# Query and key projections of ten heads in 512- and 256-column matmuls over four PSUM banks, in place of 256-column matmuls over two

## The chip, the core and the metric

The kernel runs on one core of one Trainium2 chip. The metric is device microseconds of one execution. The core has five engines that work side by side and meet through semaphores: TensorE (PE in the profile, with its weight loads as PEld) multiplies, VectorE (DVE) and ScalarE (ACT) do elementwise work, GpSimd (POOL) and SyncE (SP) mostly issue DMAs here. Matmul results land in PSUM, eight banks of 2 KB per partition (512 floats); the engines' working memory is SBUF.

## The reference, cut to what matters

Two layers over x of 256 tokens by 2048: a gated linear attention (GLA, 4 heads) and a retention layer (8 heads). Each projects the normalised input into q, k, values and gates, mixes along the tokens, normalises per head, multiplies by silu(gate), and projects back.

```python
proj = h @ w_in                       # GLA: 2048 -> 1024+1024+4096+4096, retention: 2048 -> 2048+2048+4096+4096
q, k, v, gate = jnp.split(proj, ...)
...                                   # rotary or decay, chunked scores, values, norm per head
return (o * jax.nn.silu(gate)) @ w_out   # 4096 -> 2048
h = h + mixer(rms_norm(h, norm))      # twice, then a final rms_norm
```

All inputs are float32 and the result must be accurate to about that. Nearly all of the time is these dense projections: some 320 MB of weights are read once.

## The kernel before, in words

**Precision by two halves.** Each float32 operand is split into a high half (rounded to the fp32r type of the fast matmul) and the rest. A product of two operands is then three fast matmuls: high by high, high by low, low by high. The activations live split in `xhl` (and `ogt` for the output projections): 16 blocks of 128 rows, each with a high and a low half of 256 tokens side by side, so 512 columns.

**The weight pipeline.** `_plan` lists all weight blocks in the order of use: a *sub* is 256 rows by 512 columns (512 KB, two 128-row blocks). SP loads a sub into one of 8 raw buffers; `emit_split` makes the halves, `hi` on ACT (L291) and `lo` on DVE (L292); both have 4 buffers, and the splits are issued 3 subs ahead of their use (`LOOK`).

**Pairs.** In many places two projections (a gate block g and a value block v of a head, or two neighbouring column blocks of an output projection) are computed together by a Strassen-like scheme, `pair` in the plan: quarter products P1, P2, P3, P5, P6, P7, P8, some on sums of activation blocks (`sums`, `rsum`, `osum`) and sums of weights, and plain steps v4 to v7 and g4 to g7. The sums of weights are made in the raw buffers: `post` entries of the plan are DMAs that POOL issues (L300) and that add another block onto a raw buffer after its split; `pre` entries are DVE additions (L286). A raw buffer x (g's blocks 0 and 1) serves P1, P5, P6 and P8, with additions between them; a buffer z (v's blocks 2 and 3) serves P6's sum, P3 and P7. After P6, x has g's blocks 2 and 3 added; after the later of P3 and P6, z has v's blocks 0 and 1 added. A product step P is two subs with 6 matmuls each, a plain step v or g one sub with 12.

**Orders.** A string gives the order of a pair's steps: `UNIT`, `LATE` for the first output pair of each retention half, and for the retention heads `WHOLE` (eight q steps, then UNIT; heads 0 and 4) or `MIXED` (q steps spread between the products; heads 1, 2, 3, 5, 6, 7). After each step, `turn` and `step` let one piece of the earlier head's work (`ret_tasks`: rotary, scores, values, norm, transposes) or of other side work into the program. The tile framework then lists every engine's instructions once, at build time, by its own estimate of when each is ready, so neighbouring steps can be interleaved; on the chip each engine runs its list in order.

**q and k.** A head's q and k blocks (4 column blocks of 128, numbered c) are computed transposed: the weights are the stationary operand, `xhl` the moving one. `step_w` does one sub: per 128-row block and c three matmuls of 256 columns (L365: weight high by x high; L366: weight high by x low; L368: weight low by x high), all into the same 256 columns of PSUM. So a head's q and k fill two banks (two c to a bank): for GLA heads two of the four `acc` banks (`group_w`, `evac_w`), for retention heads the two `lev` banks (`ret_head`, `qk_done`). One ACT copy of 128x512 per bank takes them out (L393, L1297). A retention pair uses the four `acc` banks as A (P1, P6, P7, P8, and the gates' second half), B (P2 and gates), C (values; in MIXED also P5) and V1 (values).

**What sets the order around the change.** In MIXED, P2 (into bank B) stands between q3 and q4. After q7 come the copies of q and k, the remaining tasks of the head before, then P3 (into C), v4, and so on.

Of the kernel before, what the change touches and what calls it, by code (L numbers as in the profile page):

```python
# [10 lines left out]
F32 = mybir.dt.float32  # L11
# [44 lines left out]
def _plan():  # L56


    loads, subs = [], []

    def load(gid, j):
        loads.append((gid, j))
        return len(loads) - 1

    def use(c, pre=None, post=()):
        subs.append((c, pre, post))

    def plain(gid, js=range(NSUB)):
        for j in js:
            use(load(gid, j))  # L70

    def pair(g, v, q=None, order=None):
        order = (order or UNIT).split()
        x = [load(g, 0), load(g, 1)] if order[0] == "P1" else []
        z = []
        later = max(("P3", "P6"), key=order.index)
        owed = []
        for n, tok in enumerate(order):
            kind, i = tok[0], tok[1:]
            if kind in "qvg":  # L80
                use(load({"q": q, "v": v, "g": g}[kind], int(i)), post=owed)
                owed = []
            elif tok == "z":
                z += [load(v, 2), load(v, 3)]
            elif tok == "P2":
                use(load(g, 2), post=owed)
                plain(g, [3])
                owed = []
            else:
                if tok == "P1" and not x:  # L90
                    x += [load(g, 0), load(g, 1)]
                for j in range(2):
                    post = []
                    if tok == later:
                        post.append((z[j], (v, j)))
                    if tok == "P1":
                        post.append((x[j], (v, j)))
                    if tok == "P6":
                        (owed if " ".join(order) == LATE else post).append((x[j], (g, 2 + j)))
                    use(z[j] if tok in ("P3", "P7") else x[j], z[j] if tok == "P6" else None, post)  # L100

    def out_cols_of(name, half, joint):
        for c in (0, 2):
# [49 lines left out]


def ret_order(h):
    return MIXED if h % 4 else WHOLE


EARLY = 2
# [10 lines left out]
def kernel(  # L170
# [17 lines left out]
    nc = tc.nc  # L188
# [9 lines left out]
    t4_p = pool("t4", 4)  # L198
# [5 lines left out]
    lev_p = pool("lev", 2, space=psum)  # L204
# [3 lines left out]
    mm = nc.tensor.matmul  # L208
    keep = tc.keep_in_program_order
# [130 lines left out]
    def steps_x(ps, lhs, js, hook=None, deadline=None):  # L340
        for j in js:
# [7 lines left out]
                hook(j)  # L349
            advance()  # L350

    def step_w(rhs, ps, j, given=True, early=False):
        hi, lo = next_weights()
        at = lambda c: ps[c // 2][:, c % 2, :]
        both = lambda c: {"skip_group_check": c % 2 == 1}
        order = [(q, c) for q in range(SUB) for c in range(4)]
        if j == NSUB - 1 or (j == 0 and given):
            order = [(q, c) for c in range(4) for q in range(SUB)]
        his, los = [], []
        for q, c in order:  # L360
            kt = j * SUB + q
            wh = hi[:, q, c * P : (c + 1) * P]
            wl = lo[:, q, c * P : (c + 1) * P]
            a = [
                lambda c=c, wh=wh, kt=kt: mm(at(c), wh, rhs[:, kt, 0, :], start=kt == 0 and c % 2 == 0, stop=False, **both(c)),  # L365
                lambda c=c, wh=wh, kt=kt: mm(at(c), wh, rhs[:, kt, 1, :], start=False, stop=False, **both(c)),  # L366
            ]
            b = [lambda c=c, wl=wl, kt=kt: mm(at(c), wl, rhs[:, kt, 0, :], start=False, stop=kt == NKT - 1, **both(c))]  # L368
            if not early:
                for x in a + b:  # L370
                    x()
                continue
            his += a
            los += b
            if c == 3:
                for x in his + los:
                    keep(x())
                his, los = [], []

    def group_w(rhs, name, extra=None, given=False):  # L380
        ps = acc(2, f"{name}_ps", (P, 2, SEQ))
# [12 lines left out]

    begun, closed = set(), set()

# [120 lines left out]
    xhl = const([P, NKT, 2, SEQ], "xhl", F32R)  # L517
# [320 lines left out]
    def gla_head(h):  # L838
        hw = {}
        if h > 1:  # L840
            side.appendleft(gla_decay(h, hw))
        ps = group_w(xhl, f"gqk{h}", None if h else first_group, h > 0)
# [6 lines left out]
        evac_w(ps, qk)  # L849
        hw["qk"] = qk  # L850
        if h == 0:
            side.append(gate_low_rank())
# [60 lines left out]
        for gi in range(2):  # L913
            g = 2 * h + gi
            if g in JOINT["a"]:
                v = v_p.tile([P, 2, 2, GW], F32R, tag="v", name=f"gv{g}")
# [4 lines left out]
                banks = [slots[n] for n in (1, 0, 2, 3)]  # L921
# [361 lines left out]
    def ret_head(h):  # L1283
        lhs = xhl
        mixed = h % 4 != 0
        at = (2, 3, 0, 1)
        q_ps = [lev_p.tile([P, 2, SEQ], F32, tag="lev", name=f"rqk{h}_ps{c}") for c in range(2)]
        r, r2 = r2_[:, 0, :], r2_[:, 1, :]
        box = {}

        def qk_done():
            if h == 0:
                token_norm(r2_, "n2")
                nc.vector.tensor_tensor(r2_[:, 1, :], r2_[:, 0, :], r2_[:, 0, :], ALU.mult)
            qk = t4_p.tile([P, 4, SEQ], F32, tag="qk", name=f"rqk{h}", bufs=1)
            for i in range(2):
                nc.scalar.activation(qk[:, 2 * i : 2 * i + 2, :], q_ps[i], AF.Copy)  # L1297
# [261 lines left out]
```

## Time and profile before

| | |
|---|---|
| median of 3 runs | 1383.21 us (1383.12 to 1383.39) |
| profiled execution, its own time | 1383.86 us |
| its span, first to last instruction | 1382.1 us, granted TensorE clock 0.998 |
| PE busy | 1369.5 us, 7376 matmuls |
| DVE busy | 1089.2 us |
| ACT busy | 847.8 us |
| POOL busy | 145.9 us |
| DMA | 321.42 MB, mean 233 GB/s |

The rows of the profile read so: the groups give line, engine, operation, tiles (out<-in), shapes and count, then busy us, mean ns of one, and idle time before them. Matmuls are pipelined, so a matmul's own length (283 ns for 256 columns) is longer than its step to the next one; the step is read from successive start times in the timeline. Timeline rows start with the start and the length in us; a bracket at the end is the idle time of that engine before the row, and what ended it. Rows of windows give the stretch, its length and each engine's busy time with the number of instructions.

### The profile page before, as it was taken

What the parts mean: (1) busy time and instruction counts of PE and PEld (TensorE: products, weight loads), DVE (VectorE), ACT (ScalarE), POOL (GpSimd) and SP (SyncE); (2) the same over time, 40 slices, a digit from 0 to 9 for tenths busy, and PEclk for the clock granted to TensorE, in tenths of its full rate; (3) what the DMA queues carried; (4) which work ended last, traced back from release to release, by engine and by line L of the source; (5) the groups of instructions that cost most, each with busy time, mean ns of one, the idle gap of its engine ahead of it and who ended that gap; (6) DMA issues with size and microseconds to landing.
All of it is one profiled execution on the core that took longest, in us unless ns stands there. A gap on an engine that the chain in (4) does not pass through costs nothing.

```text
span 1382.1 us, 19965 instructions
## 1 busy us (share of the span) xinstructions
PE 1369.5 (99%) x7376; PEld 1186.0 (86%) x7376; DVE 1089.2 (79%) x1481; ACT 847.8 (61%) x1098; POOL 145.9 (11%) x206
## 2 busy tenths in 40 slices
PE   9999999999999999999999999999999999999997
PEld 8888988888988988888989898988798989898887
DVE  6586795887778786768787888888857898987883
ACT  6576556656567756656666566665546666666662
POOL 1003020110021021001011010101101011110100
PEclk9999999999999999999999999999999999999999
DMA  9755556689658657868897879798898787979881
GB/s 345 257 182 155 182 160 196 145 253 337 210 153 257 198 175 184 318 168 240 270 328 181 270 200 282 202 329 215 243 382 222 245 237 225 261 219 280 234 291 71
DMA packets 85953, 321.42 MB, mean 233 GB/s; under 512 B 9936, under 2 KB 10960, under 8 KB 84320
## 3 DMA queue, kind: packets, MB, share of 16 engines
q1 hardware_dynamic: 66768, 240.55, 49.1%
q0 software_dynamic: 17648, 72.23, 25.0%
q10 hardware_dynamic: 1440, 7.38, 1.4%
q8 instruction: 58, 0.95, 0.3%
q14 instruction: 39, 0.32, 0.1%
HBM read 307.53 MB, written 12.58 MB: 232 GB/s over the span
## 4 chain that ended last, share of the span: by engine, by line
PE 94%; DMA 3%; DVE 1%; issue 1%; ACT 1%; POOL 0%; DVEq 0%; SPq 0%; ACTq 0%; POOLq 0%
PE re_ps L401 8%; PE re_ps L400 8%; PE re_ps L402 8%; PE rqk_ps L368 4%; PE rqk_ps L366 4%; PE rqk_ps L365 4%; DMA raw<-in_w_all 3%; PE gg_ps L332 3%; PE gv_ps L333 3%; PE gv_ps L329 3%; PE gv_ps L332 3%; PE gg_ps L329 3%; PE gg_ps L333 3%; PE gqk_ps L365 2%; PE gqk_ps L368 2%; PE gqk_ps L366 2%
## 5 line engine op out<-in xcount | busy, mean ns | idle before, releaser
L292 DVE TENSOR_TENSOR lo<-raw,hi 128x1024 fp32r<-128x1024 f32 (+1 forms) x569 | 688.7, 1221 | 222.1 <-ACT hi L291 216.6
L291 ACT ACTIVATE hi<-raw 128x1024 fp32r<-128x1024 f32 (+1 forms) x569 | 597.7, 1056 | 398.3 <-PE rqk_ps L366 61.0
L366 PE MATMUL rqk_ps<-xhl,hi 128*128 128x256 f32 x512 | 144.0, 283 | 0.0
L365 PE MATMUL rqk_ps<-xhl,hi 128*128 128x256 f32 x512 | 143.9, 283 | 0.0
L300 POOL DMA_DIRECT2D raw<-in_w_all x96 | 83.2, 867 | 547.1 <-DVE lo L292 302.7
L368 PE MATMUL rqk_ps<-xhl,lo 128*128 128x256 f32 x512 | 140.3, 283 | 0.0
L401 PE MATMUL re_ps<-lo,xhl 128*128 128x512 f32 x352 | 137.6, 391 | 0.0
L402 PE MATMUL re_ps<-hi,xhl 128*128 128x512 f32 x352 | 137.1, 389 | 0.0
L400 PE MATMUL re_ps<-hi,xhl 128*128 128x512 f32 x352 | 131.0, 390 | 0.0
L365 PEld LDWEIGHTS rqk_ps<-xhl,hi 128*128 128x128 f32 x512 | 97.9, 191 | 1.9
L366 PEld LDWEIGHTS rqk_ps<-xhl,hi 128*128 128x128 f32 x512 | 98.0, 191 | 1.4
L368 PEld LDWEIGHTS rqk_ps<-xhl,lo 128*128 128x128 f32 x512 | 96.0, 192 | 0.7
L402 PEld LDWEIGHTS re_ps<-hi,xhl 128*128 128x128 f32 x352 | 66.1, 188 | 13.3
L400 PEld LDWEIGHTS re_ps<-hi,xhl 128*128 128x128 f32 x352 | 66.2, 188 | 13.2
L401 PEld LDWEIGHTS re_ps<-lo,xhl 128*128 128x128 f32 x352 | 66.2, 188 | 12.6
L333 PE MATMUL gv_ps<-hi,xhl 128*128 128x512 f32 x192 | 75.5, 393 | 0.0
L332 PE MATMUL gg_ps<-lo,xhl 128*128 128x512 f32 x192 | 75.4, 393 | 0.0
L333 PE MATMUL gg_ps<-hi,xhl 128*128 128x512 f32 x192 | 75.0, 391 | 0.0
L332 PE MATMUL gv_ps<-lo,xhl 128*128 128x512 f32 x192 | 75.0, 391 | 0.0
L329 PE MATMUL gg_ps<-hi,xhl 128*128 128x512 f32 x192 | 74.9, 390 | 0.0
L329 PE MATMUL gv_ps<-hi,xhl 128*128 128x512 f32 x192 | 74.6, 391 | 0.0
L365 PE MATMUL gqk_ps<-xhl,hi 128*128 128x256 f32 x256 | 73.2, 289 | 1.3 <-ACT hi L291 1.3
(430 smaller groups left out, 2841.0 us busy)
## 6 DMA issues: line engine op xcount, KB each, us to landing
raw<-in_w_all SPq DMA_DIRECT2D x447, 512.0 KB, 5.2
raw<-in_w_all POOLq DMA_DIRECT2D x96, 512.0 KB, 7.5
resid<-in_x_n SPq DMA_DIRECT2D x2, 1024.0 KB, 9.5
gg<-in_gn_g POOLq DMA_DIRECT2D x8, 256.0 KB, 4.2
resid_x<-resid ACTq DMA_DIRECT2D x1, 2048.0 KB, 10.6
gb<-in_gn_b POOLq DMA_DIRECT2D x8, 256.0 KB, 7.0
gb_resid<-resid_x POOLq DMA_DIRECT2D x1, 2048.0 KB, 11.8
resid_g<-gb_resid ACTq DMA_DIRECT2D x1, 2048.0 KB, 8.8
```

Of the source, the lines that this page charges most:

```text
L291: a = nc.scalar.activation(hi[:, sl], src[:, sl], AF.Copy)
L292: b = nc.vector.tensor_tensor(lo[:, sl], src[:, sl], hi[:, sl].bitcast(F32), ALU.subtract)
L300: nc.gpsimd.dma_start(raws[n], block(key), accum_op=ALU.add)
L329: first_mm = mm(ps, xh, hi[:, q, :], start=kt == 0, stop=False)
L332: mm(ps, xh, lo[:, q, :], start=False, stop=False)
L333: mm(ps, xl, hi[:, q, :], start=False, stop=kt == NKT - 1)
L365: lambda c=c, wh=wh, kt=kt: mm(at(c), wh, rhs[:, kt, 0, :], start=kt == 0 and c % 2 == 0, stop=False, **both(c)),
L366: lambda c=c, wh=wh, kt=kt: mm(at(c), wh, rhs[:, kt, 1, :], start=False, stop=False, **both(c)),
L368: b = [lambda c=c, wl=wl, kt=kt: mm(at(c), wl, rhs[:, kt, 0, :], start=False, stop=kt == NKT - 1, **both(c))]
L400: mm(ps, xh, hi[:, q, :], start=start, stop=False, **again)
L401: mm(ps, xh, lo[:, q, :], start=False, stop=False, **again)
L402: mm(ps, xl, hi[:, q, :], start=False, stop=stop, **again)
```

## The change

It has four parts.

1. `step_w` uses the 512 columns of `xhl` (x high and x low) in one matmul with the high weights, and one matmul of 256 columns with the low weights. The result of each c is then two halves of one bank that have to be added, so q and k take four banks. This holds for all four GLA heads and retention heads 0, 1, 3, 4, 5, 7. `step_both` is the former three-matmul form, kept for retention heads 2 and 6 (`compact`).
2. The four banks: GLA head 0 takes all four `acc` banks, GLA heads 1 to 3 two `acc` and the two `lev` banks, retention heads 0 and 4 the `lev` banks, C and V1, retention heads 1, 3, 5, 7 the `lev` banks, V1 (c = 2) and B (c = 3). The evacuation is now, for each c, an ACT copy of the second half (128x256) into a `t4` tile and a DVE addition of the first half (128x256).
3. The orders: in heads 1, 3, 5, 7 (MIXED) P2 moves behind q7, because it uses B. Heads 2 and 6 keep the former string under the name SPREAD.
4. In the plan, the additions onto x after P6 are put off until the next step's first split (`owed`) in all output pairs of the retention layer; before, in the LATE pairs only. This changes one pair, the second of the first half.

```diff
                     if tok == "P6":
-                        (owed if " ".join(order) == LATE else post).append((x[j], (g, 2 + j)))
+                        (owed if v[0] == "ro" else post).append((x[j], (g, 2 + j)))
...
-MIXED = "q0 q1 P1 q2 q3 P2 q4 z P5 q5 P6 q6 q7 P3 v4 v5 v6 P7 v7 g4 g5 P8 g6 g7"
+MIXED = "q0 q1 P1 q2 q3 q4 z P5 q5 P6 q6 q7 P2 P3 v4 v5 v6 P7 v7 g4 g5 P8 g6 g7"
+SPREAD = "q0 q1 P1 q2 q3 P2 q4 z P5 q5 P6 q6 q7 P3 v4 v5 v6 P7 v7 g4 g5 P8 g6 g7"
...
-    return MIXED if h % 4 else WHOLE
+    return (WHOLE, MIXED, SPREAD, MIXED)[h % 4]
...
+    def step_both(rhs, ps, j):
+        hi, lo = next_weights()
...
+            mm(at, wh, rhs[:, kt, 0, :], start=kt == 0 and c % 2 == 0, stop=False, **more)
+            mm(at, wh, rhs[:, kt, 1, :], start=False, stop=False, **more)
+            mm(at, wl, rhs[:, kt, 0, :], start=False, stop=kt == NKT - 1, **more)
     def step_w(rhs, ps, j, given=True, early=False):
...
+            if kt == NKT - 1:
+                mm(ps[c][:, 0, :], wl, rhs[:, kt, 0, :], start=False, stop=False)
+                mm(ps[c], wh, rhs[:, kt, :, :], start=False, stop=True)
+            else:
+                mm(ps[c], wh, rhs[:, kt, :, :], start=kt == 0, stop=False)
+                mm(ps[c][:, 0, :], wl, rhs[:, kt, 0, :], start=False, stop=False)
...
+    def group_w(rhs, name, extra=None, ps=None):
+        given = ps is not None
+        ps = ps or acc(4, f"{name}_ps", (P, 2, SEQ))
...
-    def evac_w(ps, dst):
+    def evac_w(ps, dst, name):
+        tmp = t4_p.tile([P, 4, SEQ], F32, tag="t4", name=f"{name}_h2")
         with tc.high_priority():
-            for i in range(2):
-                to = dst[:, i, :].rearrange("p (z k t) -> p k z t", z=2, k=2)
-                nc.scalar.activation(to, ps[i].rearrange("p k (z t) -> p k z t", z=2), AF.Copy)
+            for c in range(4):
+                nc.scalar.activation(tmp[:, c, :], ps[c][:, 1, :], AF.Copy)
+                halves = lambda a: a.rearrange("p (z t) -> p z t", z=2)
+                to = dst[:, c // 2, :].rearrange("p (z k t) -> p z k t", z=2, k=2)[:, :, c % 2, :]
+                nc.vector.tensor_tensor(to, halves(ps[c][:, 0, :]), halves(tmp[:, c, :]), ALU.add)
...
+        if h > 0:
+            banks = acc(2, f"gqk{h}_ps", (P, 2, SEQ))
+            banks += [lev_p.tile([P, 2, SEQ], F32, tag="lev", name=f"gqk{h}_ps{c}") for c in (2, 3)]
...
+        compact = h % 4 == 2
         q_ps = [lev_p.tile([P, 2, SEQ], F32, tag="lev", name=f"rqk{h}_ps{c}") for c in range(2)]
+        if not compact:
+            more = (3, 1) if mixed else (2, 3)
+            q_ps += [acc(1, f"rqk{h}_ps{n}", (P, 2, SEQ), [at[n]])[0] for n in more]
...
-            for i in range(2):
-                nc.scalar.activation(qk[:, 2 * i : 2 * i + 2, :], q_ps[i], AF.Copy)
+            if compact:
+                for i in range(2):
+                    nc.scalar.activation(qk[:, 2 * i : 2 * i + 2, :], q_ps[i], AF.Copy)
+            else:
+                tmp = t4_p.tile([P, 4, SEQ], F32, tag="t4", name=f"rqk{h}_h2")
+                for c in range(4):
+                    nc.scalar.activation(tmp[:, c, :], q_ps[c][:, 1, :], AF.Copy)
+                    nc.vector.tensor_tensor(qk[:, c, :], q_ps[c][:, 0, :], tmp[:, c, :], ALU.add)
...
-            step_w(lhs, q_ps, j)
+            (step_both if compact else step_w)(lhs, q_ps, j)
```

More of the change, by code (lines that the diff above doesn't have):

```diff
@@ L350, in steps_x @@
             advance()
+    def step_both(rhs, ps, j):
+        hi, lo = next_weights()
+        order = [(q, c) for q in range(SUB) for c in range(4)]
+        if j in (0, NSUB - 1):
+            order = [(q, c) for c in range(4) for q in range(SUB)]
+        for q, c in order:
+            kt = j * SUB + q
+            at, more = ps[c // 2][:, c % 2, :], {"skip_group_check": c % 2 == 1}
+            wh = hi[:, q, c * P : (c + 1) * P]
+            wl = lo[:, q, c * P : (c + 1) * P]
+            mm(at, wh, rhs[:, kt, 0, :], start=kt == 0 and c % 2 == 0, stop=False, **more)
+            mm(at, wh, rhs[:, kt, 1, :], start=False, stop=False, **more)
+            mm(at, wl, rhs[:, kt, 0, :], start=False, stop=kt == NKT - 1, **more)
     def step_w(rhs, ps, j, given=True, early=False):
         hi, lo = next_weights()
-        at = lambda c: ps[c // 2][:, c % 2, :]
-        both = lambda c: {"skip_group_check": c % 2 == 1}
+        last = j == NSUB - 1
         order = [(q, c) for q in range(SUB) for c in range(4)]
-        if j == NSUB - 1 or (j == 0 and given):
+        if last or (j == 0 and given):
             order = [(q, c) for c in range(4) for q in range(SUB)]
-        his, los = [], []
+        if early:
+            for q in range(SUB):
+                kt = j * SUB + q
+                for c in range(4):
+                    keep(mm(ps[c], hi[:, q, c * P : (c + 1) * P], rhs[:, kt, :, :], start=kt == 0, stop=False))
+                for c in range(4):
+                    keep(mm(ps[c][:, 0, :], lo[:, q, c * P : (c + 1) * P], rhs[:, kt, 0, :], start=False, stop=False))
+            order = []
         for q, c in order:
@@ L363, in step_w @@
             wl = lo[:, q, c * P : (c + 1) * P]
[L364 to L381, printed above, removed]
+            if kt == NKT - 1:
[7 more added lines that the diff above has]
+        ps = ps or acc(4, f"{name}_ps", (P, 2, SEQ))
         for j in range(NSUB):
@@ L387, in group_w @@
         return ps
-    def evac_w(ps, dst):
+    def evac_w(ps, dst, name):
+        tmp = t4_p.tile([P, 4, SEQ], F32, tag="t4", name=f"{name}_h2")
         with tc.high_priority():
-            for i in range(2):
-                to = dst[:, i, :].rearrange("p (z k t) -> p k z t", z=2, k=2)
-                nc.scalar.activation(to, ps[i].rearrange("p k (z t) -> p k z t", z=2), AF.Copy)
+            for c in range(4):
+                nc.scalar.activation(tmp[:, c, :], ps[c][:, 1, :], AF.Copy)
+                halves = lambda a: a.rearrange("p (z t) -> p z t", z=2)
+                to = dst[:, c // 2, :].rearrange("p (z k t) -> p z k t", z=2, k=2)[:, :, c % 2, :]
+                nc.vector.tensor_tensor(to, halves(ps[c][:, 0, :]), halves(tmp[:, c, :]), ALU.add)
     begun, closed = set(), set()
@@ L841, in gla_head @@
             side.appendleft(gla_decay(h, hw))
-        ps = group_w(xhl, f"gqk{h}", None if h else first_group, h > 0)
+        banks = None
+        if h > 0:
+            banks = acc(2, f"gqk{h}_ps", (P, 2, SEQ))
+            banks += [lev_p.tile([P, 2, SEQ], F32, tag="lev", name=f"gqk{h}_ps{c}") for c in (2, 3)]
+        ps = group_w(xhl, f"gqk{h}", None if h else first_group, banks)
         drain_side()
@@ L848, in gla_head @@
         qk = t4_p.tile([P, 2, 2 * SEQ], F32, tag="qk", name=f"qk{h}", bufs=1)
-        evac_w(ps, qk)
+        evac_w(ps, qk, f"gqk{h}")
         hw["qk"] = qk
@@ L1295, in qk_done @@
             qk = t4_p.tile([P, 4, SEQ], F32, tag="qk", name=f"rqk{h}", bufs=1)
-            for i in range(2):
-                nc.scalar.activation(qk[:, 2 * i : 2 * i + 2, :], q_ps[i], AF.Copy)
+            if compact:
[3 more added lines that the diff above has]
+                tmp = t4_p.tile([P, 4, SEQ], F32, tag="t4", name=f"rqk{h}_h2")
+                for c in range(4):
+                    nc.scalar.activation(tmp[:, c, :], q_ps[c][:, 1, :], AF.Copy)
+                    nc.vector.tensor_tensor(qk[:, c, :], q_ps[c][:, 0, :], tmp[:, c, :], ALU.add)
             box["qk"] = qk
         def q_step(j):
-            step_w(lhs, q_ps, j)
+            (step_both if compact else step_w)(lhs, q_ps, j)
             if j == NSUB - 1:
```

## The prediction

> **What bounds the kernel now.** First the page: busy times, the chain that ended last, the groups.
>
> ```profile
> span 1382.1 us, 19965 instructions
> PE 1369.5 (99%) x7376; PEld 1186.0 (86%) x7376; DVE 1089.2 (79%) x1481; ACT 847.8 (61%) x1098; POOL 145.9 (11%) x206
> PE 94%; DMA 3%; DVE 1%; issue 1%; ACT 1%; POOL 0%; DVEq 0%; SPq 0%; ACTq 0%; POOLq 0%
> L366 PE MATMUL rqk_ps<-xhl,hi 128*128 128x256 f32 x512 | 144.0, 283 | 0.0
> ```
>
> TensorE is busy 99% and holds 94% of the chain, so a matmul saved is time saved as long as operands and banks stay ready. Then the waits of PE: two more stand there beside the start of the kernel's.
>
> ```profile
> PE rae_ps L400 <- ACT hi L291: 0.8, 1, 0.8
> PE rae_ps L400 <- DVE resid L1016: 0.4, 1, 0.4
> ```
>
> The groups' 283 ns is no rate, since matmuls overlap. The rate comes from a stretch with one kind alone: windows over q steps of retention head 3 and over a run of 512-column matmuls.
>
> ```profile
> 871.73:877.47 5.74, 5.74 (x48) 5.70 (x47) 0.00 (x0) 1.00 0.96 323
> 852.10:858.89 6.79, 6.79 (x30) 1.00 0.88 264
> ```
>
> 48 starts in 5.74 us are 0.1196 us for 256 columns; 30 in 6.79 are 0.2263 for 512. Half the columns cost more than half the time: some 13 ns per matmul go to the instruction itself.
>
> **Term 1: fewer matmuls.** Per 128-row block and c, three matmuls of 256 become one of 512 and one of 256. Ten heads of 64 such groups are 640. By the two rates a group falls from 3 x 0.1196 = 0.3588 to 0.2263 + 0.1196 = 0.3459 us, 12.9 ns, in all 8.3 us. But the new sequence alternates, and the timeline of PE has such a place in head 3:
>
> ```profile
> 913.49 0.39 PE L401 MATMUL re_ps<-lo,xhl 128*128 128x512 f32 x1
> 913.72 0.28 PE L1228 MATMUL rs<-rqs,rks 128*128 128x256 f32 x1
> 913.84 0.40 PE L402 MATMUL re_ps<-hi,xhl 128*128 128x512 f32 x1
> 914.07 0.28 PE L1229 MATMUL rs<-rqs,rks 128*128 128x256 f32 x1
> ```
>
> From 256 to 256 are 914.07 - 913.72 = 0.35 us, which leaves 8.8 ns, in all 5.6 us; from 512 to 512 are 0.35 too. Between 5.6 and 8.3 I take 7.0, as these are single changes inside runs and not a steady alternation.
>
> The Trainium skill ("TensorE: Matmul & The Clock Gate", Back-to-back issue gap) gives columns divided by 2.4 GHz plus about 2.5 ns for the step of a warm matmul. That would be 109 and 216 ns here and a saving of only 2.5 ns per group, an estimate of 1.6 us; the windows above, at full granted clock, show 120 and 226, so the trace disagrees.
>
> **Term 2: the evacuation.** Per head two ACT copies of 128x512 (587 ns in the rows of L1297) become four of 128x256, and DVE gets four additions. The nearest rows:
>
> ```profile
> L1297 ACT ACTIVATE rqk<-rqk_ps 128x512 f32<-128x512 f32 x16 | 9.4, 587 | 3.4 <-PE rqk_ps L368 3.4
> L1221 ACT ACTIVATE rks<-ra 128x256 fp32r<-128x256 f32 x8 | 3.2, 402 | 0.0
> L1128 DVE TENSOR_TENSOR resid<-tail_ps,resid 128x256 f32<-128x256 f32 x4 | 1.7, 420 | 13.3 <-PE tail_ps L333 13.3
> ```
>
> Ten heads add 40 x 0.42 = 16.8 us on DVE and 40 x 0.40 - 20 x 0.59 = 4.2 us on ACT. Both lie beside PE while the splits keep ahead; the cover is DVE's idle time. The tightest place is head 1, q0 to q7 and then P3 to g4:
>
> ```profile
> 721.42:760.96 39.54, 39.54 (x270) 36.73 (x269) 31.88 (x47) 24.54 (x34) 6.32 (x8) 1.00 0.75 206
> 760.96:779.88 18.92, 18.92 (x94) 15.84 (x93) 17.42 (x22) 11.51 (x15) 0.57 (x1) 1.00 0.82 251
> ```
>
> P2 (12 matmuls, 2.7 us of PE, two `lo` splits of 1.22 us) moves from the first stretch to the second. In the first, PE takes 39.54 - 2.7 - 0.7 = 36.1 us against DVE 31.88 - 2.4 + 1.3 = 30.8. In the second PE takes 21.6, DVE 17.42 + 2.4 + 0.8 = 20.6: 95%, still covered; without that cover it would be a wait of up to 1 us, which is the kind that term 4 counts.
>
> **Term 3: bank B.** In heads 1, 3, 5, 7 P2 follows q7 and needs B, which holds c = 3, the last to finish. At the least it waits for the last matmul's end, copy and addition: 0.39 - 0.23 + 0.40 + 0.42 and, by my estimate, 0.05 for each of three hand-overs, 1.1 us. Where P3's first sub (6 matmuls, 1.36 us, into free C) is listed ahead of P2, this is hidden. That neighbouring steps are interleaved so shows in GLA head 0, where 12 value matmuls run from 28.44 to 31.42 among those of q and k:
>
> ```profile
> 28.44 0.62 PE L329 MATMUL gv_ps<-hi,xhl 128*128 128x512 f32 x2
> 28.90 0.40 PE L365 MATMUL gqk_ps<-xhl,hi 128*128 128x256 f32 x2
> 31.42 0.28 PE L366 MATMUL gqk_ps<-xhl,hi 128*128 128x256 f32 x1
> ```
>
> What the engines do at the end of q7 in head 1, then in head 3 (timelines of PE, ACT, DVE):
>
> ```profile
> 760.84 0.28 PE L368 MATMUL rqk_ps<-xhl,lo 128*128 128x256 f32 x1
> 761.04 1.06 ACT L291 ACTIVATE hi<-raw 128x1024 fp32r<-128x1024 f32 x1 [0.72 <-PE rqk_ps L366]
> 762.01 0.58 ACT L1297 ACTIVATE rqk<-rqk_ps 128x512 f32<-128x512 f32 x1
> 759.25 1.23 DVE L292 TENSOR_TENSOR lo<-raw,hi 128x1024 fp32r<-128x1024 f32 x1 [0.30 <-ACT hi L291]
> 760.58 1.42 DVE L1263 SCALAR_TENSOR_TENSOR ro<-ro,ra,gb 128x512 f32<-128x512 f32 x2
> 765.39 1.22 DVE L1199 TENSOR_TENSOR ra<-rqk,trig 128x1024 f32<-128x1024 f32 x1
> ```
>
> ```profile
> 898.02 0.28 PE L368 MATMUL rqk_ps<-xhl,lo 128*128 128x256 f32 x1
> 899.32 1.22 DVE L292 TENSOR_TENSOR lo<-raw,hi 128x1024 fp32r<-128x1024 f32 x1 [1.66 <-ACT hi L291]
> 901.96 1.22 DVE L1199 TENSOR_TENSOR ra<-rqk,trig 128x1024 f32<-128x1024 f32 x1
> ```
>
> In head 3 (and 7) DVE sits idle for 1.66 us there: no wait. In head 1 (and 5) DVE is full, so the addition comes behind one running instruction of up to 1.23 us: 1.1 + 1.2 - 1.36 = 0.9 us. Two heads: 1.8 us. The lower end is 0, the upper is the second rival below. Heads 0 and 4 need C and V1 only after P1, 2.7 us after q7 against 1.1: nothing. That cover gone, they would cost 1.1 each.
>
> **Term 4: the addition onto z.** With P2 between q7 and P3, P3's second split needs the `hi` buffer that q7 frees; before, it was the one that P6 freed, 48 x 0.1196 = 5.7 us of q6 and q7 earlier. From it hang POOL's addition onto z and P7. The old chain in head 1 (ACT split, POOL issue, ACT's split after the landing, PE's first use), and the wait of ACT in head 3:
>
> ```profile
> 756.38 1.05 ACT L291 ACTIVATE hi<-raw 128x1024 fp32r<-128x1024 f32 x1
> 759.14 0.86 POOL L300 DMA_DIRECT2D raw<-in_w_all  x1 [1.64 <-DVE ra L506]
> 769.45 1.06 ACT L291 ACTIVATE hi<-raw 128x1024 fp32r<-128x1024 f32 x1 [2.73 <-PE rot_tp L709]
> 774.17 0.39 PE L400 MATMUL re_ps<-hi,sums 128*128 128x512 f32 x1
> ```
>
> ```profile
> 905.20 1.06 ACT L291 ACTIVATE hi<-raw 128x1024 fp32r<-128x1024 f32 x1 [2.89 <-DMA raw<-in_w_all]
> ```
>
> Old lead: 774.17 - 756.38 = 17.8 us. New: q7's end to P7 was 774.17 - 760.96 = 13.2, plus P2 2.7, less 0.4 for the copy in front, 15.5: 2.3 us lost. The old slack is 774.17 - 769.45 = 4.7 less `hi` and `lo` 2.3 = 2.4 us. So nothing is left, and nothing lost; queued behind a late z on ACT are the splits of v7 and g4. I take 0.2 us in each of four heads, 0.8 us; ends 0 and 1.2 each (the copy, the addition and one split all in front). The SP queue gets P2's two loads six places later and the loads of q4, z, q5 to q7 two earlier; POOL's order stays. P1's addition onto x has 2.7 us less before P5:
>
> ```profile
> raw<-in_w_all POOLq DMA_DIRECT2D x96, 512.0 KB, 7.5
> ```
>
> Between its split and P5's still lie q2, q3, q4 and a product sub, 3 x 24 x 0.1196 + 1.36 = 10.0 us at the old rate, 9.8 at the new, against 7.5 from issue to landing: nothing.
>
> **Term 5: GLA head 0** takes all four `acc` banks, so value steps can no longer fill its q steps, as those 12 matmuls did. What q waited for is on DVE:
>
> ```profile
> 27.64 1.67 DVE L559 SCALAR_TENSOR_TENSOR xhl<-xt,smalls,xhl 128x256 fp32r<-128x256 f32 x4
> ```
>
> The last four x blocks are done at 27.64 + 1.67 = 29.31, the value matmuls began at 28.44: at most 0.9 us, and q6 needs the blocks one by one, 0.42 us apart: 0.3. Other GLA heads: their `lev` banks are idle in q steps, nothing; at worst 4 x 0.42 us of additions in front of the scores, for which PE has no wait in its list.
>
> **Term 6: `owed`.** Chain and POOL at the one pair it touches, the place of PE's two waits:
>
> ```profile
> 986.44 1.15 DVE raw L286
> 988.10 8.22 DMA raw<-in_w_all
> 996.43 1.07 ACT hi L291
> ```
>
> ```profile
> 988.10 1.76 POOL L300 DMA_DIRECT2D raw<-in_w_all  x2 [1.38 <-DVE raw L286]
> ```
>
> The issue at 988.10 follows the addition that reads z's second buffer (986.44 to 987.59), so it is z's, ahead of x's at 988.10 + 0.88: I cost it at nothing. Lower end: the whole stall gone, 0.8 + 0.4 = 1.2 us gained.
>
> **Sum.** -7.0 + 1.8 + 0.8 + 0.3 = -4.1 us against the profiled 1382.1 span (1383.86 with what lies around it), so -4.1 against the median 1383.21: 1379.1 us.
>
> **Rivals.** (a) *The waits eat the gain.* DVE's first look at q and k came 765.39 - 760.84 = 4.55 us (head 1) and 901.96 - 898.02 = 3.94 us (head 3) after the last q matmul. If B's addition takes that place, B is free after 5.0 and 4.4 us; P3's two subs cover 2.7: 2 x 2.3 + 2 x 1.7 = 8.0. With 1.1 for terms 4 and 5: 1383.2 - 7.0 + 8.0 + 1.1 = 1385.3, no change. Against it: the additions stand ahead of those tasks in the program.
>
> (b) *Slower: P2 in strict order.* The same late addition with nothing listed between q7 and P2: 2 x 5.0 + 2 x 4.4 = 18.8 us, 1383.2 - 7.0 + 18.8 + 1.1 = 1396.1. It decides for slower from (7.0 - 1.1 + 2.8) / 4 = 2.2 us of wait per head. Against it: the interleaving in GLA head 0.
>
> (c) *The instruction's cost is not saved.* If in a steady alternation the 512 took as long as the two 256 that it replaces, 2 x 0.1196, term 1 is zero: 1383.2 + 2.9 = 1386.1. Against it: the row pairs of 0.35 us. By the Trainium skill's formula in term 1 its gain would be 1.6 us, with the same waits 1384.5.
>
> **Numbers.** Forecast 0.58, (a) 0.24, (b) 0.15, (c) 0.03. Within 0.2% (1380.4 to 1386.0) is about what a measurement can tell from no change. Faster 0.58, same 0.24, slower 0.18. Range: low -8.3 without waits and without the stall, 1383.2 - 8.3 - 1.2 = 1373.7; high (a) with half a microsecond more, 1385.8; (b) and (c) stay out. The forecast's own range is 1373.7 to 1380.4.
>
> **What would show it.** PE with 640 matmuls fewer, groups of q and k at about 0.35 us; DVE up by 17 us; at the end of q7 in heads 1 and 5 P3 ahead of P2 or a gap of about 1 us, none in 3 and 7; P7's `hi` split right behind z's landing; 988's stall unchanged. Wrong: gaps of over 2 us at P2, or a pair of matmuls at 0.36.

## The result and the profile after

The changed kernel takes 1387.9 us (median of 13 runs, 1385.83 to 1392.16) against 1383.01 us before (13 runs beside it, 1381.97 to 1383.51). The ratio is 1.0037, 95% interval 1.0028 to 1.0046: slower by some 5 us, where 4 us were forecast as a gain. The profiled execution took 1387.9 us, with a span of 1386.1 us against 1382.1 before.

From the page of the changed kernel (span, busy times) and from its list of PE's waits (us in total, times, longest):

```profile
span 1386.1 us, 18745 instructions
PE 1366.5 (99%) x6736; PEld 1151.6 (83%) x6736; DVE 1104.1 (80%) x1521; ACT 851.7 (61%) x1118; POOL 145.5 (10%) x206
```

```profile
PE re_ps L416 <- ACT hi L292: 3.9, 4, 1.3
PE re_ps L417 <- DVE lo L293: 3.0, 4, 0.8
```

PE has its 640 matmuls fewer and VectorE is up by 15 us, as forecast. But two rows are new at the top of the waits: PE waits in the products `re_ps<-hi,sums`, four times for `hi` and four times for `lo`, 6.9 us. All eight lie in P7 of retention heads 2 and 6. Those are the two heads (with the order `SPREAD`) that keep the 256-column form and their old order of steps; not a line of their own work was changed.

The chain of the changed kernel in head 2 shows what P7 waited for (start, duration, piece):

```profile
825.16 12.42 DMA raw<-in_w_all
...
837.68 1.06 ACT hi L292
...
838.77 1.24 DVE lo L293
...
840.05 0.50 PE re_ps L417
```

This transfer is one of POOL's two additions of v onto z. It took 12.42 us from issue to landing. POOL's timelines at this place, first of the kernel before, then of the changed one, show why (start, duration, out<-in, and in brackets the idle time ahead and what ended it):

```profile
826.82 0.86 POOL L300 DMA_DIRECT2D raw<-in_w_all  x1 [4.90 <-DVE lo L292]
828.72 0.86 POOL L300 DMA_DIRECT2D raw<-in_w_all  x1 [1.04 <-DVE lo L292]
831.27 0.56 POOL L440 DMA_DIRECT2D rsum_kept<-rsum_t  x1 [1.69 <-DVE rsum_t L473]
836.23 0.55 POOL L440 DMA_DIRECT2D rsum_kept<-rsum_t  x1 [4.40 <-DVE rsum_t L473]
```

```profile
820.90 0.56 POOL L456 DMA_DIRECT2D rsum_kept<-rsum_t  x1 [0.90 <-DVE rsum_t L489]
822.70 0.55 POOL L456 DMA_DIRECT2D rsum_kept<-rsum_t  x1 [1.24 <-DVE rsum_t L489]
825.16 1.83 POOL L301 DMA_DIRECT2D raw<-in_w_all  x2 [1.90 <-DVE lo L293]
```

`rsum_kept<-rsum_t` are the two transfers of `spill_sums`, 512 KB each, which put half of the sums for the output product away until head 3 (and 7). Before, they were issued behind z's two additions; now they are issued ahead of them. The additions themselves are issued 1.7 to 2.6 us earlier than before on each trace's own time, but the spills stand in front: z's blocks land 12.4 and 15.3 us after issue, against 5.6 and 8.1 us before. The DMA engines have little room to spare in either kernel. The views of DMA from 815 to 845 us show it, before and then after: first the busy share of the 16 DMA engines in 40 slices, in tenths, then the issues (transfers, KB each, median us to landing).

```profile
DMA  0056830939999997999999989999999999998069
raw<-in_w_all POOLq DMA_DIRECT2D x4, 512.0 KB, 5.8
```

```profile
DMA  0976009699989999999999999999999995769204
raw<-in_w_all POOLq DMA_DIRECT2D x4, 512.0 KB, 10.7
rsum_kept<-rsum_t POOLq DMA_DIRECT2D x2, 512.0 KB, 10.1
```

In head 6 a lower granted clock follows the waits. Windows of the changed kernel, the first over the waits of head 6, the second right behind it, the third over the waits of head 2 (PE, PEld, DVE, ACT, POOL busy, then the granted clock, DMA share, GB/s):

```profile
1197.97:1201.38 3.41, 1.55 (x7) 0.86 (x6) 2.09 (x3) 2.00 (x2) 0.00 (x0) 1.00 0.40 142
1201.38:1204.80 3.42, 3.42 (x12) 2.95 (x11) 3.42 (x5) 3.05 (x5) 0.00 (x0) 0.50 0.82 193
839.57:842.98 3.41, 1.82 (x6) 1.05 (x6) 2.04 (x4) 1.50 (x2) 0.00 (x0) 1.00 0.71 216
```

The clock falls to half for 3.4 us, although PE's work is there again; behind the waits of head 2 it stays at 1.00.

The two traces add up, when the time between the starts of neighbouring matmuls is compared with 0.227 us for 512 columns and 0.120 for 256: -6.0 us for the fewer matmuls, +5.0 at P7 of head 2, +4.1 at P7 of head 6, +1.7 for matmuls at the lower clock behind it, -1.8 for the stall near 998 us, which is gone, and +0.9 at two small stalls in the GLA output pairs. That is +3.9 us; the spans differ by 4.0.

### The profile page after: what moved, and what is told of

Its sections match the earlier page's. It is cut to its first block, busy times and chain, and to the rows that moved or that the text cites. A ratio compares the mean times of both kernels' runs of the same rounds, so it can differ in the third digit from the quotient of the medians.

```text
span 1386.1 us, 18745 instructions
## 1 busy us (share of the span) xinstructions
PE 1366.5 (99%) x6736; PEld 1151.6 (83%) x6736; DVE 1104.1 (80%) x1521; ACT 851.7 (61%) x1118; POOL 145.5 (10%) x206
## 4 chain that ended last, share of the span: by engine, by line
PE 77%; issue 13%; DMA 6%; DVE 2%; POOL 1%; ACT 1%; POOLq 0%; DVEq 0%; SPq 0%; ACTq 0%
DMA raw<-in_w_all 6%; PE rqk_ps L389 5%; PE re_ps L417 5%; PE re_ps L418 5%; PE re_ps L416 5%; PE gqk_ps L389 4%; PE gg_ps L333 3%; PE gv_ps L334 3%; PE gv_ps L333 3%; PE gv_ps L330 3%; PE gg_ps L330 3%; PE gg_ps L334 3%; PE rqk_ps L390 2%; PE ge_ps L417 2%; PE ge_ps L416 2%
## 5 line engine op out<-in xcount | busy, mean ns | idle before, releaser
L389 PE MATMUL rqk_ps<-xhl,hi 128*128 128x512 f32 x360 | 123.3, 397 | 0.0
L390 PE MATMUL rqk_ps<-xhl,lo 128*128 128x256 f32 x360 | 93.7, 282 | 0.0
L389 PEld LDWEIGHTS rqk_ps<-xhl,hi 128*128 128x128 f32 x360 | 66.7, 188 | 13.3
L416 PEld LDWEIGHTS re_ps<-hi,xhl 128*128 128x128 f32 x352 | 66.4, 189 | 13.5
L389 PE MATMUL gqk_ps<-xhl,hi 128*128 128x512 f32 x216 | 76.5, 398 | 0.0
L390 PEld LDWEIGHTS rqk_ps<-xhl,lo 128*128 128x128 f32 x360 | 66.0, 189 | 2.7
L847 POOL TENSOR_TENSOR s<-s,m 128x64 f32<-128x64 f32 x56 | 36.1, 676 | 232.9 <-DVE m L838 223.6
L390 PE MATMUL gqk_ps<-xhl,lo 128*128 128x256 f32 x216 | 59.0, 280 | 0.0
## 6 DMA issues: line engine op xcount, KB each, us to landing
gb_resid<-resid_x POOLq DMA_DIRECT2D x1, 2048.0 KB, 11.7
```

The costliest lines, as they stand in the source:

```text
L389: mm(ps[c], wh, rhs[:, kt, :, :], start=kt == 0, stop=False)
L390: mm(ps[c][:, 0, :], wl, rhs[:, kt, 0, :], start=False, stop=False)
L416: mm(ps, xh, hi[:, q, :], start=start, stop=False, **again)
L847: nc.gpsimd.tensor_tensor(dst, dst, side_of(m[:, li, :], z), ALU.add)
```

## The experiments

Theory T1: the order of the spills and z's additions in heads 2 and 6 is the whole loss. Rivals: T2, there are too many transfers at that time whatever their order; T3, VectorE's added work makes the split late on which z's additions wait. The 12 runs, of 5 to 12 executions each:

| run | time, us | kernel before beside it | ratio, 95% interval |
|---|---|---|---|
| e_spill_late | 1380.14 | 1383.0 | 0.9979 (0.9970 to 0.9988) |
| e_spill_act | 1382.0 | 1383.0 | 0.9995 (0.9986 to 1.0004) |
| e_before_order | 1382.18 | 1383.0 | 0.9991 (0.9983 to 1.0000) |
| e_before_owed | 1383.63 | 1383.0 | 1.0002 (0.9994 to 1.0011) |
| e_gla_whole | 1379.56 | 1383.79 | 0.9973 (0.9963 to 0.9982) |
| e_mixed_only | 1390.32 | 1383.79 | 1.0050 (1.0036 to 1.0063) |
| e_best | 1377.09 | 1383.79 | 0.9953 (0.9940 to 0.9965) |
| e_best2 | 1378.96 | 1383.79 | 0.9965 (0.9954 to 0.9977) |
| e_no_p2_step | 1376.66 | 1383.1 | 0.9959 (0.9947 to 0.9972) |
| e_mixed_late | 1382.39 | 1383.1 | 0.9996 (0.9987 to 1.0005) |
| e_before_best | 1383.94 | 1383.1 | 1.0006 (0.9997 to 1.0015) |
| e_no_p2_best | 1378.65 | 1383.1 | 0.9968 (0.9957 to 0.9980) |

### The spills behind z's additions

```diff
             if making and tok in ("q3", "P2", "q4", "P5", "q5"):
                 next(making)
-                if tok == "q5":
-                    spill_sums(f"rsum{h}")
+            if making and tok == "q7":
+                spill_sums(f"rsum{h}")
 ...
-            nc.gpsimd.dma_start(
+            keep(nc.gpsimd.dma_start(
```

> The changed kernel with one edit: in retention heads 2 and 6 the two spill transfers rsum_kept<-rsum_t (0.5 MB each) are issued behind the two additions of v onto z, as in the kernel before, and not ahead of them. Theory T1 (the spills, ahead of the additions, make z land 12.4 and 15.3 us after issue instead of 5.6 and 8.1, and P7 waits): no wait of PE at P7 of heads 2 and 6 above 0.3 us, z's additions land 5 to 9 us after issue, time 1387.9 - 4.8 - 3.9 = 1379.2 us, down to 1376 if the lower clock of head 6 goes too. Rival T2 (the transfers as a whole are too many at that time, the order is no matter): waits at P7 stay at 3 us or more a head, 1386 to 1388.5 us. Rival T3 (z is late because VectorE's added work makes its split late): the same, 1386 to 1388.5 us.

(`keep` holds an instruction at its place in the program's order.) Measured: 1380.14 us, 0.9 us above the 1379.2 expected; ratio 0.9979, against 1.0037 for the change as it stands. One edit that moves two transfers is worth 0.0058 of the time, 8 us, and turns the change from a loss into a gain. POOL's timeline in head 2:

```profile
824.34 0.86 POOL L301 DMA_DIRECT2D raw<-in_w_all  x1 [4.97 <-DVE lo L293]
825.65 0.85 POOL L301 DMA_DIRECT2D raw<-in_w_all  x1 [0.44 <-DVE lo L293]
826.18 1.43 POOL L456 DMA_DIRECT2D rsum_kept<-rsum_t  x2
```

Two rows of its chain there, and the only row of PE's waits that lies in heads 2 and 6:

```profile
826.73 14.56 DMA rsum_kept<-rsum_t
...
841.32 0.42 ACT rks L1241
```

```profile
PE rs L1247 <- ACT rks L1241: 1.7, 2, 0.9
```

The waits of P7 are out of the list (0.4 us a head is left in the intervals between starts). T2 and T3 fall: the same transfers and the same work on VectorE are there. z's second block still lands 10.5 us after its issue, so these transfers still crowd each other; what the order decides here is who waits. Now it is the spill, 14.56 us, and the buffer that it holds back: `rks` of the scores takes the tile that `rsum_t` leaves, and PE waits 0.9 us for it in each of the two heads.

### The spills in another queue

```diff
-            nc.gpsimd.dma_start(
-                kept[:, i * QK * 2 * P : (i + 1) * QK * 2 * P], cur["next_s"][2 + i].rearrange("p k a t -> p (k a t)")
+            nc.scalar.dma_start(
+                kept[:, i * QK * 2 * P : (i + 1) * QK * 2 * P].bitcast(F32), cur["next_s"][2 + i].rearrange("p k a t -> p (k a t)").bitcast(F32)
```

> The changed kernel with one edit: the two spill transfers of heads 2 and 6 are issued by ACT into its own queue and not by POOL into the software queue; the rest stays. If it is the order inside the one software queue that holds z back (T1a), z's additions land 5 to 9 us after issue and the time falls to 1377 to 1380 us. If it is the transfer time that the spills take from all 16 DMA engines (T1b), z's additions still land 10 us or more after issue and 3 to 5 us of waits at P7 stay in each of the two heads: 1384 to 1388 us.

Measured: 1382.0 us, between the two expectations, with a wide spread: ten of the 12 executions took 1379.58 to 1382.61 us, the others 1385.13 and 1388.02. By the ratios (0.9995 against 1.0037 and 0.9979) a queue of its own for the spills takes back 5.8 of the 8.0 us that the order takes back. The trace is of the slowest execution, in which two falls of the granted clock, of the kind told in the last section, cost some 3.4 us more. In it the waits are still there, 4.4 us instead of 6.9, and the transfers hardly faster (waits of PE; DMA issues from 815 to 845 us):

```profile
PE re_ps L417 <- DVE lo L293: 2.3, 4, 0.8
PE re_ps L416 <- ACT hi L292: 2.1, 2, 1.1
```

```profile
raw<-in_w_all POOLq DMA_DIRECT2D x4, 512.0 KB, 10.2
rsum_kept<-rsum_t ACTq DMA_DIRECT2D x2, 512.0 KB, 9.2
```

In this execution z's blocks land 10.7 and 13.2 us after issue; it is 12.4 and 15.3 with the spills ahead in the same queue and 6.1 and 10.5 with the spills behind. So about 2 us of this delay come from standing behind the spills in one queue, and the rest goes with having the spills under way at the same time, whatever queue they are in. The Trainium skill ("DMA: Bandwidth & Descriptors", Issuing engines are not separate DMA queues) says that transfers started by different engines run on the same 16 DMA engines and interleave; these landings agree. The ten faster executions left no trace. By their times most of the wait is gone in them, and why the second queue helps there and so little here stays open.

### Which part of the change turned the order

The change in two halves, both with the old condition of `owed`. First the GLA heads and heads 0 and 4 alone, then heads 1, 3, 5 and 7 alone:

```diff
-    return (WHOLE, MIXED, SPREAD, MIXED)[h % 4]
+    return SPREAD if h % 4 else WHOLE
 ...
-        compact = h % 4 == 2
+        compact = h % 4 != 0
```

> One part of the change alone: the 512- and 256-column form in the four GLA heads and in retention heads 0 and 4; heads 1, 3, 5, 7 keep the 256-column form and P2 ahead of q4, and the handing on of additions is the old one. POOL keeps the old order in heads 2 and 6 (z's additions ahead of the spills). T1: 6 x 64 groups x 9.4 ns (350 against 359.4 ns, from the alternation in the changed kernel's trace) = 3.6 us gained and no wait at P7: 1379.4 us. If the evacuation's additions on VectorE cost something in these heads: 1381 us or more.

Measured: 1379.56 us, ratio 0.9973. Six heads in the new form gain 3.7 us (2.5 to 5.1) where 3.6 were expected; 40% of the new matmul form is left out, and it beats the whole by 9 us.

```diff
     # group_w, step_w and evac_w of the kernel before for the GLA heads
-        compact = h % 4 == 2
+        compact = h % 2 == 0
```

> The other part alone: the 512- and 256-column form with P2 behind q7 in retention heads 1, 3, 5, 7; GLA heads and heads 0 and 4 as before. Here POOL's order turns (spills ahead of z's additions in heads 2 and 6). T1: 4 x 64 groups x 9.4 ns = 2.4 us gained, 4 to 5 us of waits at P7 lost in each of heads 2 and 6, and up to 2 us to a lower granted clock behind them: 1388 to 1392 us, slower than the whole change. If the waits come from the whole change together and not from heads 1 and 5 ahead of heads 2 and 6: 1380.6 us.

Measured: 1390.32 us (5 executions), ratio 1.0050: this half alone costs more than the whole. Its list of waits shows the same two rows at the same place:

```profile
PE re_ps L440 <- ACT hi L292: 3.3, 4, 1.2
PE re_ps L441 <- DVE lo L293: 3.0, 4, 0.8
```

The same half with the spills held behind z's additions, by the edit shown first:

> The form in heads 1, 3, 5, 7 alone (measured as 1390.3 us) with the spills held behind z's additions. T1: the whole loss was the order of the transfers; with it gone the form shows its 2.4 us, less the 2.2 us that late spills cost at heads 2 and 6 in the first experiment: 1381 to 1383 us. If heads 1, 3, 5, 7 lose time in other ways (waits for bank B, VectorE): 1385 us or more.

Measured: 1382.39 us, ratio 0.9996. The order is again worth 0.0054, 7.5 us, and what is left, -0.6 us (-1.8 to 0.7), is the 2.4 us of fewer matmuls less the waits that late spills bring (1.6 us at the scores, as in the first experiment). Heads 1, 3, 5 and 7 lose nothing of their own that this interval could show.

Is it the place of P2, without the form?

```diff
+SPREAD = "q0 q1 P1 q2 q3 P2 q4 z P5 q5 P6 q6 q7 P3 v4 v5 v6 P7 v7 g4 g5 P8 g6 g7"
-MIXED = "q0 q1 P1 q2 q3 P2 q4 z P5 q5 P6 q6 q7 P3 v4 v5 v6 P7 v7 g4 g5 P8 g6 g7"
+MIXED = "q0 q1 P1 q2 q3 q4 z P5 q5 P6 q6 q7 P2 P3 v4 v5 v6 P7 v7 g4 g5 P8 g6 g7"
 ...
-    return MIXED if h % 4 else WHOLE
+    return (WHOLE, MIXED, SPREAD, MIXED)[h % 4]
```

> The kernel before with P2 moved behind q7 in retention heads 1, 3, 5, 7 and nothing else (q and k in 256-column matmuls in all heads). There is no wait for a bank in this form. If the place of P2 alone turned the order of spills and z's additions in heads 2 and 6, P7 waits there and the time is 1386 to 1392 us. If it takes the 512-column form, the order of the transfers stays as before and the time is 1382.5 to 1384.5 us (the stall of 1.7 us near 998 stays).

Measured: 1382.18 us, ratio 0.9991 (to 1.0000): the order of the transfers stays the old one and nothing is lost. What moves is when the sums are ready. VectorE's last write of `rsum_t` in head 2, and the last write of head 1's output into `ogt`, from which the sums are made: before, then with the order alone, then with the whole change.

```profile
818.33 1.28 DVE L717 TENSOR_TENSOR ogt<-rot_tp,ogt 128x512 fp32r<-128x512 f32 x2
...
835.25 0.69 DVE L473 TENSOR_TENSOR rsum_t<-rsum_f,rsum_t 128x512 fp32r<-128x512 f32 x1
```

```profile
815.48 0.68 DVE L718 TENSOR_TENSOR ogt<-rot_tp,ogt 128x512 fp32r<-128x512 f32 x1
...
829.37 0.69 DVE L474 TENSOR_TENSOR rsum_t<-rsum_f,rsum_t 128x512 fp32r<-128x512 f32 x1
```

```profile
805.95 1.29 DVE L733 TENSOR_TENSOR ogt<-rot_tp,ogt 128x512 fp32r<-128x512 f32 x2 [0.66 <-ACT ogt L732]
...
821.71 0.70 DVE L489 TENSOR_TENSOR rsum_t<-rsum_f,rsum_t 128x512 fp32r<-128x512 f32 x1
```

The sums are ready 5.9 us earlier by the order alone and 13.5 us earlier by the whole change, of which 1.7 us in both is the lead that z's first addition has too. With the order alone the first spill is issued at 827.51 us, half a microsecond behind the second addition (826.98); with the whole change the spills are ahead of z's additions in POOL's list. That list is made at build time, by the framework's estimate of when each instruction is ready; the measured times stand in for the estimate here. A reason that the code shows: `turn` takes one step of a head's own output work after each token behind q7, but P7, g4 and g5. P2 stood ahead of q7 and now stands behind it, so the heads 1, 3, 5 and 7 have nine such places and not eight, and their output runs one place earlier. The next run takes that place away again.

```diff
-                if tok not in ("P7", "g4", "g5"):
+                if tok not in (("P7", "g4", "g5") if compact else ("P2", "P7", "g4", "g5")):
                     step()
```

> The changed kernel with one edit: in heads 1, 3, 5, 7 the turn behind P2 no longer takes a step of the head's own output work (with P2 behind q7 that turn had become one step more than before). Theory: that step, together with the form, brings the head's output and so head 2's and 6's sums forward, and with them the spills ahead of z's additions. Without it POOL's old order returns by itself: no wait at P7 above 0.5 us, 1377 to 1380 us. If the step is not what did it, waits at P7 of 3 us or more a head: 1386 to 1389 us.

Measured: 1376.66 us (1376.38 to 1377.55), ratio 0.9959. This is just below the 1377 to 1380 us expected. POOL's timeline in head 2 has the old order with nothing pinned, and the longest rows of PE's waits have none in heads 2 and 6. The third view is VectorE's last write of `rsum_t`:

```profile
822.30 0.86 POOL L301 DMA_DIRECT2D raw<-in_w_all  x1 [4.87 <-DVE lo L293]
823.60 0.85 POOL L301 DMA_DIRECT2D raw<-in_w_all  x1 [0.45 <-DVE lo L293]
828.69 0.56 POOL L456 DMA_DIRECT2D rsum_kept<-rsum_t  x1 [4.24 <-DVE rsum_t L489]
831.84 0.55 POOL L456 DMA_DIRECT2D rsum_kept<-rsum_t  x1 [2.59 <-DVE rsum_t L489]
```

```profile
PE warm_ps L551 <- POOL warm L549: 1.8, 1, 1.8
PE gqk_ps L377 <- ACT hi L292: 1.3, 1, 1.3
PE rae_ps L416 <- DVE resid L1036: 0.4, 1, 0.4
```

```profile
830.86 0.68 DVE L489 TENSOR_TENSOR rsum_t<-rsum_f,rsum_t 128x512 fp32r<-128x512 f32 x1
```

Without the extra place the sums come 4.4 us earlier than in the kernel before, and z's first addition 4.5 us earlier (822.30 against 826.82): the form alone moves nothing between them. The order alone brings the sums some 4 us nearer to z's additions, and both together some 12 us. So the one more place for a step in heads 1, 3, 5 and 7, together with the form, set off the waits in heads 2 and 6; why the two bring so much more together than each alone was not followed further. With that place taken away the change gains 5.7 us (3.9 to 7.3), which agrees with its 6.0 us of fewer matmuls.

### `owed` alone

```diff
-                        (owed if " ".join(order) == LATE else post).append((x[j], (g, 2 + j)))
+                        (owed if v[0] == "ro" else post).append((x[j], (g, 2 + j)))
```

> The kernel before with the one changed condition of the additions that are handed on (all output pairs of the retention halves). By term 6 nothing: 1383.0 us. If the stall of 0.97 + 0.69 us near 998 goes with it: 1381.3 us.

Measured: 1383.63 us, ratio 1.0002, no difference. The wait `rae_ps` for `hi` near 998 us is still there with 0.5 us (0.8 before); it is absent with the order alone, which keeps the old `owed`. So `owed` is not what took the stall away in the changed kernel, and of its two waits `e_no_p2_step` has the one for `resid`, 0.4 us, again.

### Towards the fastest form

The waits at the scores that late spills bring should go when the scores come one step later in heads 2 and 6; P7's own margin grows when it follows v7:

```diff
-SPREAD = "q0 q1 P1 q2 q3 P2 q4 z P5 q5 P6 q6 q7 P3 v4 v5 v6 P7 v7 g4 g5 P8 g6 g7"
+SPREAD = "q0 q1 P1 q2 q3 P2 q4 z P5 q5 P6 q6 q7 P3 v4 v5 v6 v7 P7 g4 g5 P8 g6 g7"
 ...
-                if tok not in ("P7", "g4", "g5"):
+                if tok not in ("P3" if compact else "P7", "g4", "g5"):
```

> The changed kernel with the spills behind z's additions (as in the first experiment), and in heads 2 and 6 P7 after v7 and the steps of the scores one place later. The waits that the first experiment left there (0.3 + 0.1 us at P7, 1.0 us at the scores' matmuls that wait for the second spill's buffer, in each of two heads) should go: 1380.1 - 2.8 = 1377.3 us. If the scores' wait only moves on to what hangs from them: 1379 to 1380.5 us.

Measured: 1377.09 us, ratio 0.9953: as expected, and neither row is in the list of waits. Without the move of P7:

> As the run before it, but with P7 where it was, ahead of v7: only the scores' steps come later. The 1.0 us at the scores should go in each of two heads, P7's 0.4 us stay: 1380.1 - 2.0 = 1378.1 us. If the scores' wait only moves on: 1379 to 1380.5 us.

Measured: 1378.96 us, ratio 0.9965, 0.9 us above what was expected; the scores' wait is gone, 1.2 us of P7's are back. The same edits without the change:

> The kernel before with the edits of the best version to heads 2 and 6 (spills held behind z's additions, P7 after v7, the scores one step later) and nothing of the change. If the best version's time is the change's gain, this one stays near the kernel before, 1382.5 to 1384 us. If heads 2 and 6 gain by those edits in any form, 1380 to 1382 us.

Measured: 1383.94 us, ratio 1.0006. So the edits only take away what the change had brought. And the two ways together, no step at P2, P7 and the scores later, the spills free:

> The changed kernel without the step behind P2 in heads 1, 3, 5, 7, and with P7 after v7 and the scores one step later in heads 2 and 6; the spills are not held, they come behind z's additions by themselves. If the waits left by the held spills were due to their early time, this is the fastest form: 1376 to 1377.5 us; if not, 1377 to 1379 us.

Measured: 1378.65 us, ratio 0.9968, at the upper end of the second expectation. There was no wait left in heads 2 and 6 that the later steps could have taken away, so they brought nothing. The lowest times are those of `e_no_p2_step` and `e_best`, 5 executions each. Their intervals overlap with each other and with those of `e_best2` and `e_no_p2_best`, so none of the four is shown to be the fastest; `e_no_p2_step` needs one line.

## Why the prediction was wrong

- **Term 1, fewer matmuls: right in kind, in the lower half of its bounds.** The alternation is in the changed kernel's timeline of PE in head 1:

```profile
744.81 0.40 PE L389 MATMUL rqk_ps<-xhl,hi 128*128 128x512 f32 x1
745.04 0.28 PE L390 MATMUL rqk_ps<-xhl,lo 128*128 128x256 f32 x1
745.16 0.40 PE L389 MATMUL rqk_ps<-xhl,hi 128*128 128x512 f32 x1
```

  A group takes 0.35 us, by the median over the trace 233 + 117 = 350 ns against 359, so 640 groups give 6.0 us and not 7.0: the row pairs of 0.35 us were the better guide than the run rates. Rival (c) is out; `e_no_p2_step` shows 5.7 us in the end-to-end time. The formula of the Trainium skill ("TensorE: Matmul & The Clock Gate", Back-to-back issue gap), which the page gives for an isolated matmul, would have left an estimated 1.6 us; these runs show more.
- **Term 2, the evacuation: right.** VectorE's busy time is up by 14.9 us (16.8 forecast) and ACT's by 3.9 (4.2); `e_gla_whole`, with six of these ten heads, has no wait at the evacuation.
- **Term 3, bank B: forecast 1.8 us, measured nothing.** The list put P3's first six matmuls ahead of P2, as the term assumed, and the additions came in time. PE and VectorE at the end of q7 in head 1:

```profile
754.38 0.40 PE L387 MATMUL rqk_ps<-xhl,hi 128*128 128x512 f32 x1
754.61 0.40 PE L416 MATMUL re_ps<-hi,sums 128*128 128x512 f32 x1
...
755.99 0.39 PE L416 MATMUL re_ps<-hi,xhl 128*128 128x512 f32 x1
```

```profile
754.18 0.75 DVE L1327 TENSOR_TENSOR rqk<-rqk_ps,rqk_h 128x256 f32<-128x256 f32 x2
754.91 0.75 DVE L1327 TENSOR_TENSOR rqk<-rqk_ps,rqk_h 128x256 f32<-128x256 f32 x2
```

  The last addition ends at 755.66, P2 starts at 755.99. In q7 the four c finish one after the other, so only the last copy and addition wait for the last matmuls. Rivals (a) and (b), which rested on this wait, did not come; that the time landed near (a)'s is chance.
- **Term 4, the addition onto z: this is the step that failed.** It followed z's chain in heads 1, 3, 5 and 7, where no wait appeared (0.8 us forecast, 0 measured), and said of the move that "POOL's order stays". It counted the transfers that P2's move passes, but not the step of a head's other work that `turn` takes after P2 as after most tokens. That step and the form brought head 1's output forward by about 12 us, with it head 2's sums, and POOL's order in head 2 turned. The sum had no term for heads 2 and 6 at all, as their code stands unchanged. There, P7's second split had a margin of only 0.4 us in the trace of before (0.8 us in head 6; from the end of `lo` to its first matmul), which the prediction did not consider. VectorE and PE before, in head 2:

```profile
840.17 1.29 DVE L1199 TENSOR_TENSOR rb<-rqk,trig 128x512 f32<-128x512 f32 x2 [1.96 <-DMA rsum_kept<-rsum_t]
841.38 2.35 DVE L292 TENSOR_TENSOR lo<-raw,hi 128x1024 fp32r<-128x1024 f32 x2
```

```profile
842.97 0.39 PE L401 MATMUL re_ps<-lo,sums 128*128 128x512 f32 x1
```

  P7's `lo` is the first of the two, done at about 842.6. It stood behind an `rb` that waited for a spill to land, so the spills bore on P7 already before the change. The missing term measured +9.1 us of waits and +1.7 us at a lower clock in the profiled execution, and about 8 us in the times by `e_spill_late`.
- **Term 5, GLA head 0: 0.3 us forecast, no wait seen.** PE's list has the same wait there as before, 1.2 us against 1.3.
- **Term 6, `owed`: right**, nothing by itself. The stall near 998 us went all the same, and in `e_before_order` it goes with the order of steps alone.

## What to carry to other kernels

When a step is moved in a written order, list everything that is counted by steps, the work of a neighbour that advances once per step too, and follow where that work's transfers then stand in their queue. A transfer that came ready late and is now ready early is not a gain if it goes ahead of one that is urgent: here the order of issue in one queue cost 8 us, and another queue for the less urgent transfers took back 5.8 of them. Look up the stages with the least margin in the old trace first, in unchanged parts as well: waits of 5 us arose where the margin was 0.4.

## What was not expected of the hardware

Waits of at most 1.3 us each, spread over six microseconds (1195 to 1201 us), were followed in head 6 by a granted clock of 0.50 for 3.41 us (1201.38 to 1204.80), with PE at work again; nearly the same waits in head 2, and those of `e_mixed_only`'s profiled execution in both heads, left it at 1.00. In `e_spill_act`'s trace the clock fell for 3.41 us in both heads, at 843.84 and 1202.24 us, 358.40 us apart, which is 105 times 3.413. In all 14 traces of this case the changes of the granted clock are whole multiples of 3.413 us apart, and the first comes at another place in each, 8.3 to 11.7 us from the start.

As far as these traces show, it depends on how busy PE was in the stretch of 3.41 us ahead of such a point, and not on the longest wait. Cut into such stretches, the 14 traces have their least busy ones right ahead of the three falls: PE is busy there for 1.55, 1.54 and 1.70 us. All other stretches but those at the very end have at least 1.72, head 2's above 1.82 and `e_mixed_only`'s 1.94 and 1.95. Three falls give no exact limit, and the busy time of PE is in part modelled. But nearly the same waits can cost 1.7 us more or nothing, by where the stretches happen to lie. The clocks of the executions without a trace fit: of the 13 executions of the changed kernel twelve have a mean granted clock of 0.993 (the slowest, 1392.16 us) to 0.997 and one 0.999, and all those of the kernel before beside the experiments 0.998 or 0.999.

The Trainium skill ("TensorE: Matmul & The Clock Gate", What's actually happening) has the clock fall after an idle window of about 3.4 us that runs freely of the kernel. The traces agree with the length and with windows that run freely; but the windows ahead of the falls were not idle, PE was busy in them for 45 to 50% of the time.
